# Between the two layers: more buffers for split weights, two weight splits inside the layer norm's chain, the keys' blocks split behind the queries', and the root's first guess in one operation

## The chip, the cores and the metric

The kernel runs on one core of one Trainium2 chip. The metric is the device time of one execution in microseconds (us). The kernel before takes 1261.22 us, the median of 3 runs (1261.05 to 1261.33). Its profile comes from one execution that took 1262.22 us itself.

## The reference

256 tokens of width 2048 pass through two layers in fp32. Layer 0 is a Mamba-2 SSD mixer, layer 1 a sparse-attention mixer with a lightning indexer. After each mixer comes a post-norm residual:

```
x = layer_norm(ALPHA * x + mixer(x), g, b)      # ALPHA = 4 ** 0.25
# layer 1 begins with
proj = x @ w_in                                  # 2048 -> 512 | 256 | 64 | 16 | 4096
c_q, c_kv, k_idx, w_idx, gate = split(proj)
c_q  = rms_norm(c_q, q_norm_g)                   # 512 columns, "queries"
c_kv = rms_norm(c_kv, kv_norm_g)                 # 256 columns, "keys"
```

Every product keeps fp32 precision: an operand is split into a rounded part `hi` and a remainder `lo`, and a product is made as hi·hi, hi·lo and lo·hi.

## The kernel before

**A stream of weight units.** `Stream` holds some 400 units of weights, each a tile of 128 x 1024 (128 x 672 for the keys), numbered in the order of use. `load` issues the DMA of unit i on SyncE's queue into one of 4 raw buffers. `convert` makes the two parts: ScalarE copies raw to `hi` with rounding (L98), VectorE subtracts to get `lo` (L99), and then the load of unit i + 4 is issued, into the raw buffer that the subtraction has just freed. `run` keeps the splits up to 4 units ahead of the matmuls; `limit` holds that back. The parts live in two pools of 4 buffers; a table `homes` sends single units to another pool, `wmore`, which in this kernel has 4 buffers of each part.

**The order is written out by hand.** Each engine executes its instructions in the order in which the program issues them, and waits on semaphores between engines. Nothing is scheduled by costs; what is issued first on an engine stands first in its queue, and a waiting instruction holds all behind it.

**Between the layers.** Units 160 to 223 are the output projection of layer 0 (`o1`), in four column blocks n of 512. Its last six units (218 to 223, `held`) are first multiplied for the token half 0 alone, so that the layer norm of half 0 can start on VectorE while TensorE does half 1 of those six. Units 224 to 231 (`wcq`) are the queries' projection, units 232 to 239 (`wkv`) the keys', and then come the gates' units (`wg`). The queries' units, too, are multiplied for half 0 first (`qp0`, six matmuls a unit) and, after all eight, for half 1 (`qp1`); the parts of all eight stay until then. `tail1` (L951) is issued with the last unit of `o1`, `early` (L973) after the matmuls of each queries' unit kb of half 0.

For one half the norm is this chain on VectorE: the residual of the last column block (L535), statistics (L538, L608, L609), the inverse root by an integer shift (L191), a guess (L193) and three steps of two operations each (L196, L198), and the normalization of four blocks of 512 columns in place (L927). Then TensorE transposes the half in four groups q of 512 columns (`turn`, tiles `x1t`), ScalarE applies gain and bias (`put`, L941, into tiles `x1f`), and each group is split into `x1T`: hi on ScalarE (L947) or VectorE (L945), lo on VectorE (L949). `x1T` is what the queries', keys' and gates' matmuls read. A name such as x1t10 means half 1, group 0; lo228 is the lo part of unit 228, the fifth queries' unit (kb 4).

After the queries comes `lat_norm` (copies of `qp`, statistics, its own root at L182), while TensorE multiplies the keys' units (tile `kvp`).

The kernel's end (`last`, L1039) is another layer norm of the same kind, whose root steps alternate with the operations that center the four blocks (L1056).

Of the kernel before, what the change touches and what calls it, by code (L numbers as in the profile page):

```python
# [53 lines left out]
LAST = 8  # L54
AHEAD = 2

# [8 lines left out]
class Stream:  # L65


    def __init__(self, nc, wraw, whi, wlo):
        self.nc, self.wraw, self.whi, self.wlo = nc, wraw, whi, wlo
        self.units, self.starts, self.active = [], {}, []  # L70
        self.raws, self.parts = {}, {}
        self.pos = self.ready = 0
        self.limit = 1 << 30
        self.homes = {}
# [14 lines left out]

    def convert(self, i, eng):  # L90

        if i < len(self.units):
            w = self.units[i].width
            r = self.raws.pop(i)
            ph, pl = (self.homes[i],) * 2 if i in self.homes else (self.whi, self.wlo)
            h = ph.tile([P, 1024], F32R, tag="hi", name=f"hi{i}")
            l = pl.tile([P, 1024], F32R, tag="lo", name=f"lo{i}")
            self.nc.scalar.activation(h[:, :w], r[:, :w], AF.Copy)  # L98
            eng.tensor_sub(l[:, :w], r[:, :w], h[:, :w].bitcast(F32))  # L99
            self.parts[i] = (h, l)  # L100
# [24 lines left out]
def trunk_kernel(ctx: ExitStack, tc: tile.TileContext, x, xt, w1, wdt, dtp, prm, wo1,  # L125
# [53 lines left out]
    def rsqrt(pool, dst, val, n, w, tag):  # L179

        t = pool.tile([n, w], F32, tag=tag, name=tag)
        v.tensor_scalar(t.bitcast(I32), val.bitcast(I32), 1, None, op0=ALU.logical_shift_right)  # L182
        v.tensor_scalar(dst.bitcast(I32), t.bitcast(I32), -1, MAGIC, op0=ALU.mult, op1=ALU.add)
        for k in range(3):
            v.tensor_mul(t, dst, dst)
            v.scalar_tensor_tensor(t, t, -0.5, val, op0=ALU.mult, op1=ALU.mult)
            v.scalar_tensor_tensor(dst, t, 1.5, dst, op0=ALU.add, op1=ALU.mult)

    def rsqrt1_steps(dst, val, t):

        v.tensor_scalar(t.bitcast(I32), val.bitcast(I32), 1, None, op0=ALU.logical_shift_right)  # L191
        yield
        v.tensor_scalar(dst.bitcast(I32), t.bitcast(I32), -1, MAGIC1, op0=ALU.mult, op1=ALU.add)  # L193
        for a in (A0, A1, A2):
# [419 lines left out]
    def stream_tok(kb, width, cell, name, held=None):  # L614
# [12 lines left out]
        def pe(h, l):  # L627
# [35 lines left out]
    def lat_norm(cell, width, g0, nt, name, dst):  # L663
# [4 lines left out]
        rs = d1.tile([P, 2], F32, tag=name + "r", name=name + "r")  # L668
        ps, tok, dst = cell["ps"], A[name], A[dst]
        for half in range(2):  # L670
# [12 lines left out]
        for q in range(nt // 2):  # L683
# [7 lines left out]
            for k in range(2):  # L691
                kt = 2 * q + k
                gs = par[:, g0 + kt:g0 + kt + 1]
                hi, lo = dst[:, kt, 0:T], dst[:, kt, T:2 * T]
                nc.scalar.activation(hi, pm[:, k * T:(k + 1) * T], AF.Copy, scale=gs)
# [221 lines left out]
    def normed(half, between=()):  # L917
# [18 lines left out]
    def put(half, q):  # L936
        t = d1.tile([P, 4, P], F32, tag="x1f", name=f"x1f{half}{q}", bufs=2)
        for j in range(4):
# [12 lines left out]
    def tail1(cell, held, mm):  # L951
# [41 lines left out]
    def area(*shape):  # L993
# [5 lines left out]
        elif len(shape) == 3:  # L999
# [4 lines left out]
             cb=area(384))  # L1004
    ckvT = d1.tile([P, 2, 2 * T], F32R, tag="ckvT", name="ckvT")
    cqT = d1.tile([P, 4, 2 * T], F32R, tag="cqT", name="cqT")
    A.update(ckvT=ckvT, cqT=cqT)
    mb = d1.tile([P, 384], F32, tag="mb", name="mb")
    nc.gpsimd.memset(A["cb"], 0.0)
# [177 lines left out]
```

## Time and profile before

| | |
|---|---|
| median of 3 runs | 1261.22 us |
| profiled execution | 1262.22 us |
| its span, first to last instruction | 1260.5 us |
| TensorE busy | 1235.4 us, 98% |
| VectorE busy | 909.4 us, 72% |
| ScalarE busy | 692.3 us, 55% |
| mean granted TensorE clock | 0.994 |
| stretch between the layers | about 670 to 732 us |

An idle time is printed in square brackets in front of the instruction that ended it, with what released it. Matmuls are pipelined, so that their durations overlap: how long one costs the engine is read from the distance between two starts. [...]

### The profile page before, as it was taken

How to read it: one execution, taken by the hardware profiler on the slowest of the kernel's cores; microseconds unless marked ns; L12 is line 12 of the kernel's file. 1: busy time of each engine (PE TensorE's matmuls, PEld its weight loads, DVE VectorE, ACT ScalarE, POOL GpSimd, SP SyncE). 2: the span in 40 equal slices, each digit the busy share in tenths (PEclk: the TensorE clock that was granted, in tenths of full speed). 3: DMA queues.
4: the chain of work that ended last, by engine and by line, in shares of the span. 5: the costliest groups of instructions: out<-in, count | busy, mean ns of one | idle time of the engine just before them, and what ended most of it. 6: DMA issues, size and time to landing. Idle time of an engine off the chain costs nothing.

```text
span 1260.5 us, 19096 instructions
## 1 busy us (share of the span) xinstructions
PE 1235.4 (98%) x7066; PEld 1072.6 (85%) x7066; DVE 909.4 (72%) x1685; ACT 692.3 (55%) x1186; POOL 68.6 (5%) x104
## 2 busy tenths in 40 slices
PE   8999999999999999999998999999999999999996
PEld 6888888888888888788887798999999999888885
DVE  6978788888889889757457568856666666567457
ACT  5566566666656666444435455566566666433340
POOL 1001001100110010110001000000000000000000
PEclk9999999999999999999999999999999999999998
DMA  7766657565656565676664464544444444965662
GB/s 273 207 189 184 205 177 216 156 214 178 215 167 208 184 203 171 193 255 192 202 198 159 157 225 149 185 152 149 160 159 145 154 149 151 352 204 185 200 197 86
DMA packets 65292, 236.51 MB, mean 188 GB/s; under 512 B 7912, under 2 KB 7920, under 8 KB 64816
## 3 DMA queue, kind: packets, MB, share of 16 engines
q1 hardware_dynamic: 60192, 215.12, 53.8%
q0 software_dynamic: 5008, 20.19, 5.0%
q8 instruction: 55, 0.90, 0.3%
q14 instruction: 37, 0.30, 0.1%
HBM read 231.00 MB, written 4.28 MB: 187 GB/s over the span
## 4 chain that ended last, share of the span: by engine, by line
PE 93%; DVE 4%; DMA 1%; issue 1%; ACT 0%; SPq 0%; DVEq 0%; ACTq 0%
PE acc L267 22%; PE acc L271 11%; PE g L267 9%; PE o L497 9%; PE o L499 9%; PE o L498 9%; PE g L271 5%; PE y L395 2%; DVE lo L99 1%; PE q L822 1%; PE q L823 1%; PE q L824 1%; PE lg L840 1%; PE o L871 1%; PE pt L864 1%; DMA scr<-in_xt_dram 1%
## 5 line engine op out<-in xcount | busy, mean ns | idle before, releaser
L99 DVE TENSOR_TENSOR lo<-raw,hi 128x1024 fp32r<-128x1024 f32 (+1 forms) x404 | 489.2, 1214 | 279.4 <-ACT hi L98 279.2
L98 ACT ACTIVATE hi<-raw 128x1024 fp32r<-128x1024 f32 (+1 forms) x404 | 421.2, 1049 | 219.6 <-PE o L499 163.0
L267 PE MATMUL acc<-xT,hi 128*128 128x512 f32 x1280 | 324.7, 395 | 0.0
L267 PEld LDWEIGHTS acc<-xT,hi 128*128 128x128 f32 x1280 | 230.3, 189 | 43.0 <-ACT E L350 0.9
L271 PEld LDWEIGHTS acc<-xT,lo 128*128 128x128 f32 x1280 | 174.5, 190 | 12.8
L271 PE MATMUL acc<-xT,lo 128*128 128x256 f32 x1280 | 178.3, 282 | 0.0
L267 PE MATMUL g<-x1T,hi 128*128 128x512 f32 x512 | 134.2, 404 | 0.0
L267 PEld LDWEIGHTS g<-x1T,hi 128*128 128x128 f32 x512 | 92.8, 188 | 17.9
L497 PE MATMUL o<-hi,yg 128*128 128x512 f32 x256 | 100.5, 393 | 0.8 <-DVE zs L278 0.8
L498 PE MATMUL o<-lo,yg 128*128 128x512 f32 x256 | 99.7, 389 | 0.0
L499 PE MATMUL o<-hi,yg 128*128 128x512 f32 x256 | 99.7, 389 | 0.0
L497 PE MATMUL o<-hi,og 128*128 128x512 f32 (+1 forms) x256 | 99.5, 389 | 0.0
L499 PE MATMUL o<-hi,og 128*128 128x512 f32 (+1 forms) x256 | 98.9, 386 | 0.0
L498 PE MATMUL o<-lo,og 128*128 128x512 f32 (+1 forms) x256 | 98.8, 386 | 0.0
L271 PEld LDWEIGHTS g<-x1T,lo 128*128 128x128 f32 x512 | 69.8, 190 | 5.1
L297 DVE SCALAR_TENSOR_TENSOR ca<-cr,convh,ca 128x255 f32<-128x255 f32 x144 | 69.3, 481 | 3.4
L271 PE MATMUL g<-x1T,lo 128*128 128x256 f32 x512 | 71.3, 282 | 0.0
L300 ACT ACTIVATE cr<-ca 128x256 f32<-128x256 f32 x48 | 20.1, 418 | 88.1 <-DVE ca L297 88.1
L497 PEld LDWEIGHTS o<-hi,yg 128*128 128x128 f32 x256 | 48.0, 188 | 11.2 <-ACT hi L98 1.3
L499 PEld LDWEIGHTS o<-hi,yg 128*128 128x128 f32 x256 | 48.1, 188 | 10.1
L498 PEld LDWEIGHTS o<-lo,yg 128*128 128x128 f32 x256 | 48.1, 188 | 9.9
L499 PEld LDWEIGHTS o<-hi,og 128*128 128x128 f32 x256 | 48.1, 188 | 9.9
(240 smaller groups left out, 1694.6 us busy)
## 6 DMA issues: line engine op xcount, KB each, us to landing
raw<-in_w_dram SPq DMA_DIRECT2D x160, 512.0 KB, 4.1
raw<-in_wo_dram SPq DMA_DIRECT2D x128, 512.0 KB, 4.3
raw<-in_wg_dram SPq DMA_DIRECT2D x64, 512.0 KB, 3.3
raw<-in_wab_dram SPq DMA_DIRECT2D x32, 512.0 KB, 3.3
abc<-acs_d POOLq DMA_DIRECT2D x32, 256.0 KB, 4.3
raw<-in_wcq_dram SPq DMA_DIRECT2D x8, 512.0 KB, 4.4
raw<-in_wkv_dram SPq DMA_DIRECT2D x8, 336.0 KB, 5.7
rx<-in_x_dram POOLq DMA_DIRECT2D x2, 1024.0 KB, 11.8
```

The costliest lines, as they stand in the source:

```text
L98: self.nc.scalar.activation(h[:, :w], r[:, :w], AF.Copy)
L99: eng.tensor_sub(l[:, :w], r[:, :w], h[:, :w].bitcast(F32))
L267: nc.tensor.matmul(ps, h[:, k * P:(k + 1) * P], xs[:, kt, :], start=(kt == 0), stop=False, skip_group_check=True)
L271: nc.tensor.matmul(ps[:, 0:T], l[:, k * P:(k + 1) * P], xs[:, kt, 0:T], start=False, stop=(kt == 15), skip_group_check=True)
L297: v.scalar_tensor_tensor(acc[:, d:], rw[:, :T - d], w(k), acc[:, d:], op0=ALU.mult, op1=ALU.add)
L300: nc.scalar.activation(rw, acc, AF.Tanh)
L395: nc.tensor.matmul(py[ks, c * T + s * P:(c + 1) * T], xsT[:, s, c, ks], ms[c][k][:, ws], start=(c == 0 and s == 0), stop=(s == 1), skip_gr ...
L497: nc.tensor.matmul(ps, ah, hs, start=(kk == 2 * first), stop=False)
L498: nc.tensor.matmul(ps, ah, ls, start=False, stop=False)
L499: nc.tensor.matmul(ps, al, hs, start=False, stop=(kk == 31))
L822: nc.tensor.matmul(ps, h[:, o:o + P], cqT[:, kt, 0:T], start=(kt == 0), stop=False)
L823: nc.tensor.matmul(ps, h[:, o:o + P], cqT[:, kt, T:2 * T], start=False, stop=False)
```

## The change

It consists of six edits.

1. `wmore` gets 6 buffers of each part in place of 4, and holds units 222 to 227, then 232 and 233; `AHEAD` grows from 2 to 4, so that units 226 and 227 may be split before and at the head of `tail1`. The space for it comes from the `x1f` tiles, which now lie in the dead part of the residual's input, and from `ckvT`, `cqT` and `mb`, which are made later, in a pool `lat` opened once `wmore` is closed.
2. In `tail1` units 228 and 229 are split on either side of the residual of half 1, and 230 and 231 inside the norm of half 1: `start` issues the ScalarE part, `finish` the VectorE part and the load. `convert` is cut in two for that.
3. The normalization of half 1 is shared: blocks 0 and 2 on VectorE, 1 and 3 on ScalarE, with a new one-column operation for the bias (`nm`).
4. The hi parts of the transposed groups 0 and 1 are made on VectorE, of 2 and 3 on ScalarE (before: 1 and 3, 0 and 2).
5. The transposes of half 1 stand behind the seventh and eighth queries' unit (kb 6 and 7) in place of the sixth and seventh; the first two keys' units are split ahead of that half's groups, and two more right behind the queries, ahead of `lat_norm`.
6. The root's shift and guess become one operation (val x -0.5 + constant on the integer view), in both root functions, so also at the kernel's end.

```diff
-AHEAD = 2
+AHEAD = 4
...
-    def convert(self, i, eng):
+    def convert(self, i, eng, later=False):
...
             self.nc.scalar.activation(h[:, :w], r[:, :w], AF.Copy)
-            eng.tensor_sub(l[:, :w], r[:, :w], h[:, :w].bitcast(F32))
             self.parts[i] = (h, l)
+            self.halfway[i] = (l[:, :w], r[:, :w], h[:, :w].bitcast(F32))
+        if not later:
+            self.finish(i, eng)
+
+    def finish(self, i, eng):
+        if i in self.halfway:
+            eng.tensor_sub(*self.halfway.pop(i))
         self.load(i + RAW)
...
-        v.tensor_scalar(t.bitcast(I32), val.bitcast(I32), 1, None, op0=ALU.logical_shift_right)
-        yield
-        v.tensor_scalar(dst.bitcast(I32), t.bitcast(I32), -1, MAGIC1, op0=ALU.mult, op1=ALU.add)
+        v.tensor_scalar(dst.bitcast(I32), val.bitcast(I32), -0.5, MAGIC1, op0=ALU.mult,
+                        op1=ALU.add)
...
-    wmore = between.enter_context(tc.tile_pool(name="wmore", bufs=4))
-    for i in (n_o1 - 2, n_o1 - 1, n_o1, n_o1 + 1, n_o1 + 6, n_o1 + 7):
-        st.homes[i] = wmore
+    wmore = between.enter_context(tc.tile_pool(name="wmore", bufs=6))
+    for i in (-2, -1, 0, 1, 2, 3, 8, 9):
+        st.homes[n_o1 + i] = wmore
...
                 for a in held:
                     mm(*a, 1)
+                st.limit = 1 << 30
+                st.convert_to(n_o1 + EARLY + 4)
...
+        nm = d1.tile([P, 1], F32, tag="nm", name="nm")
+        v.scalar_tensor_tensor(nm, mv[:, 0:1], -1.0, rs, op0=ALU.mult, op1=ALU.mult)
         for n in range(4):
             s = L["r"][:, half, n * 512:(n + 1) * 512]
-            v.tensor_scalar(s, s, mv[:, 0:1], rs, op0=ALU.subtract, op1=ALU.mult)
+            if n % 2:
+                nc.scalar.activation(s, s, AF.Identity, scale=rs, bias=nm)
+            else:
+                v.tensor_scalar(s, s, mv[:, 0:1], rs, op0=ALU.subtract, op1=ALU.mult)
...
-        if q % 2:
+        if q < 2:
             v.tensor_copy(hi, t)
...
-        st.limit = n_o1 + EARLY
-        st.convert_to(n_o1 + 3)
+        st.limit = n_o1 + EARLY + 2
+        st.convert_to(n_o1 + AHEAD)
         now(put(0, 0))
         now(put(0, 1))
-        st.convert_to(n_o1 + 4)
+        st.convert_to(n_o1 + AHEAD + 1)
         now(residual(3, 1, cell))
+        st.convert_to(n_o1 + 6)
         p2, p3 = put(0, 2), put(0, 3)
-        normed(1, (p2, p2, p3, p3))
+
+        def split():
+            st.start(n_o1 + 6)
+            st.start(n_o1 + 7)
+            yield
+            st.finish(n_o1 + 6, v)
+        normed(1, (p2, p2, p3, p3, split()))
+        st.finish(n_o1 + 7, v)
```

VectorE's queue, from the end of half 1's root on, before; `rx` holds the residual stream, `mv1` and `rs1` mean and inverse root of half 1:

```order
L196 TENSOR_SCALAR t1_6920<-rs1_6918,ve1_6919 128x1
L198 SCALAR_TENSOR_TENSOR rs1_6918<-t1_6920,rs1_6918 128x1
L927 TENSOR_SCALAR rx_6159<-rx_6159,mv1_6917,rs1_6918 128x512 x4
L99 TENSOR_TENSOR lo228_6970<-raw228_6784,hi228_6969 128x1024
L99 TENSOR_TENSOR lo229_6982<-raw229_6796,hi229_6981 128x1024
L99 TENSOR_TENSOR lo230_6994<-raw230_6892,hi230_6993 128x1024
L99 TENSOR_TENSOR lo231_7006<-raw231_6912,hi231_7005 128x1024
L949 TENSOR_TENSOR x1T_6831<-x1f10_7033,x1T_6831 128x4x128
```

Lo228 to lo231 stand behind the whole norm of half 1. The same place now, the end of half 1's root on VectorE:

```order
L207 TENSOR_SCALAR t1_6925<-rs1_6923,ve1_6924 128x1
L209 SCALAR_TENSOR_TENSOR rs1_6923<-t1_6925,rs1_6923 128x1
L106 TENSOR_TENSOR lo230_6945<-raw230_6804,hi230_6944 128x1024
L946 SCALAR_TENSOR_TENSOR nm_6956<-mv1_6922,rs1_6923 128x1
L952 TENSOR_SCALAR rx_6155<-rx_6155,mv1_6922,rs1_6923 128x512 x2
L106 TENSOR_TENSOR lo231_6948<-raw231_6893,hi231_6947 128x1024
L106 TENSOR_TENSOR lo232_7007<-raw232_6911,hi232_7006 128x672
L106 TENSOR_TENSOR lo233_7019<-raw233_6920,hi233_7018 128x672
L970 CAST x1T_6832<-rx_6155 128x4x128
L974 TENSOR_TENSOR x1T_6832<-rx_6155,x1T_6832 128x4x128
```

Lo228 and lo229 have moved ahead of the root, lo230 stands between root and normalization, and the first two keys' units stand ahead of the first group of half 1. VectorE at the residual of half 0, before; `o1_3_0` is the last column block's sum for half 0:

```order
L99 TENSOR_TENSOR lo225_6793<-raw225_6748,hi225_6792 128x1024
L535 SCALAR_TENSOR_TENSOR rx_6159<-rx_6159,o1_3_0_6568 128x512
L538 BN_STATS st1_6160<-rx_6159 128x6 x2
L608 BN_AGGR mv0_6813<-st1_6160 128x2
L609 TENSOR_SCALAR ve0_6815<-mv0_6813 128x1
L191 TENSOR_SCALAR t0_6816<-ve0_6815 128x1
L193 TENSOR_SCALAR rs0_6814<-t0_6816 128x1
```

and now:

```order
L106 TENSOR_TENSOR lo225_6789<-raw225_6744,hi225_6788 128x1024
L106 TENSOR_TENSOR lo226_6801<-raw226_6756,hi226_6800 128x1024
L546 SCALAR_TENSOR_TENSOR rx_6155<-rx_6155,o1_3_0_6564 128x512
L549 BN_STATS st1_6156<-rx_6155 128x6 x2
L621 BN_AGGR mv0_6815<-st1_6156 128x2
L622 TENSOR_SCALAR ve0_6817<-mv0_6815 128x1
L203 TENSOR_SCALAR rs0_6816<-ve0_6817 128x1
```

Lo226 has moved ahead of the residual, from behind the normalization of half 0, and the root begins with one operation. Further on, between that normalization and the residual of half 1, VectorE now has lo227, two casts, two subtractions and lo228, where it had lo226, lo227, one cast and two subtractions; lo229 stands right behind the residual's statistics. ScalarE around half 1's groups, before (`x1t10` is the transposed group 0 of half 1):

```order
L98 ACTIVATE hi228_6969<-raw228_6784 128x1024
L98 ACTIVATE hi229_6981<-raw229_6796 128x1024
L98 ACTIVATE hi230_6993<-raw230_6892 128x1024
L98 ACTIVATE hi231_7005<-raw231_6912 128x1024
L941 ACTIVATE x1f10_7033<-x1t10_7023,par_88 128x128 x4
L947 ACTIVATE x1T_6831<-x1f10_7033 128x4x128
```

and now (the target `rx` of L966 is the `x1f` of before):

```order
L98 ACTIVATE hi230_6944<-raw230_6804 128x1024
L98 ACTIVATE hi231_6947<-raw231_6893 128x1024
L950 ACTIVATE rx_6155<-rx_6155,nm_6956,rs1_6923 128x512 x2
L98 ACTIVATE hi232_7006<-raw232_6911 128x672
L98 ACTIVATE hi233_7018<-raw233_6920 128x672
L966 ACTIVATE rx_6155<-x1t10_7030,par_88 128x128 x4
```

The two operations of the normalization and the keys' two splits now stand between hi231 and the first group. On TensorE the only difference is that x1t10 and x1t11 stand behind unit 230 and x1t12 and x1t13 behind unit 231, right ahead of `qp1`.

## Rows read from the trace of the kernel before

**Rows 1.** The page, part 1: busy time of each engine, share, instructions.
```profile
PE 1235.4 (98%) x7066; PEld 1072.6 (85%) x7066; DVE 909.4 (72%) x1685; ACT 692.3 (55%) x1186; POOL 68.6 (5%) x104
```

**Rows 2.** Who TensorE waited for, 500 to 800 us: total us, times, longest.
```profile
PE qp L624 <- DVE lo L99: 4.2, 1, 4.2
PE kvp L623 <- ACT hi L98: 1.3, 1, 1.3
```

**Rows 3.** Windows: length, each engine's busy us (instructions), granted clock, DMA share, GB/s.
```profile
688.50:692.75 4.25, 0.00 (x2) 0.00 (x1) 4.07 (x12) 1.95 (x3) 0.57 (x1) 0.85 0.00 0
692.75:697.60 4.85, 4.85 (x11) 3.68 (x12) 3.35 (x3) 0.00 (x0) 0.00 (x0) 0.50 0.99 382
713.50:716.20 2.70, 0.89 (x3) 0.44 (x3) 1.82 (x3) 2.45 (x4) 0.00 (x0) 1.00 0.00 0
```

**Rows 4.** Timeline of TensorE: start, us, operation, count, idle before and releaser.
```profile
678.06 1.03 PE L933 MATMUL x1t<-ident,rx 128*128 128x128 f32 x8
678.85 0.48 PE L497 MATMUL o<-hi,yg 128*128 128x512 f32 x1
...
682.59 0.40 PE L623 MATMUL qp<-hi,x1T 128*128 128x512 f32 x1
...
688.11 0.39 PE L623 MATMUL qp<-hi,x1T 128*128 128x512 f32 x1
692.75 0.79 PE L624 MATMUL qp<-lo,x1T 128*128 128x512 f32 x1 [4.25 <-DVE lo L99]
...
697.61 1.37 PE L933 MATMUL x1t<-ident,rx 128*128 128x128 f32 x8
698.73 0.48 PE L623 MATMUL qp<-hi,x1T 128*128 128x512 f32 x1
```

**Rows 5.** Timeline of TensorE from the last queries' matmul to the keys' first.
```profile
713.32 0.40 PE L625 MATMUL qp<-hi,x1T 128*128 128x512 f32 x1
715.05 0.42 PE L623 MATMUL kvp<-hi,x1T 128*128 128x336 f32 x1 [1.34 <-ACT hi L98]
715.95 0.42 PE L624 MATMUL kvp<-lo,x1T 128*128 128x336 f32 x1 [0.47 <-DVE lo L99]
```

**Rows 6.** Timeline of VectorE between the layers.
```profile
672.79 0.69 DVE L535 SCALAR_TENSOR_TENSOR rx<-rx,o 128x512 f32<-128x512 f32 x1 [0.27 <-PE o L499]
...
676.79 1.92 DVE L927 TENSOR_SCALAR rx<-rx,mv,rs 128x512 f32<-128x512 f32 x4
...
684.50 0.68 DVE L535 SCALAR_TENSOR_TENSOR rx<-rx,o 128x512 f32<-128x512 f32 x1
...
687.33 0.42 DVE L945 CAST x1T<-x1f 128x512 fp32r<-128x512 f32 x1
...
689.64 1.92 DVE L927 TENSOR_SCALAR rx<-rx,mv,rs 128x512 f32<-128x512 f32 x4
691.48 4.62 DVE L99 TENSOR_TENSOR lo<-raw,hi 128x1024 fp32r<-128x1024 f32 x4
700.78 0.69 DVE L949 TENSOR_TENSOR x1T<-x1f,x1T 128x512 fp32r<-128x512 f32 x1 [4.68 <-ACT x1T L947]
```

**Rows 7.** Timeline of ScalarE between the layers.
```profile
670.20 1.06 ACT L98 ACTIVATE hi<-raw 128x1024 fp32r<-128x1024 f32 x1 [1.58 <-DMA raw<-in_wcq_dram]
674.17 1.06 ACT L98 ACTIVATE hi<-raw 128x1024 fp32r<-128x1024 f32 x1 [2.91 <-PE o L499]
678.69 1.51 ACT L941 ACTIVATE x1f<-x1t,par 128x128 f32<-128x128 f32 x4 [3.46 <-PE x1t L933]
...
700.12 0.63 ACT L947 ACTIVATE x1T<-x1f 128x512 fp32r<-128x512 f32 x1
...
714.25 2.71 ACT L98 ACTIVATE hi<-raw 128x672 fp32r<-128x672 f32 x4
```

**Rows 8.** The chain that ended last, at the kernel's end: start, us, operation.
```profile
1250.34 0.17 DVE t L191
1250.53 0.15 DVE rs L193
```

More of the change, by code (lines that the diff above doesn't have):

```diff
@@ L70, in __init__ @@
         self.units, self.starts, self.active = [], {}, []
-        self.raws, self.parts = {}, {}
+        self.raws, self.parts, self.halfway = {}, {}, {}
         self.pos = self.ready = 0
@@ L98, in convert, with start @@
             self.nc.scalar.activation(h[:, :w], r[:, :w], AF.Copy)
-            eng.tensor_sub(l[:, :w], r[:, :w], h[:, :w].bitcast(F32))
             self.parts[i] = (h, l)
+            self.halfway[i] = (l[:, :w], r[:, :w], h[:, :w].bitcast(F32))
[4 more added lines that the diff above has]
+            eng.tensor_sub(*self.halfway.pop(i))
         self.load(i + RAW)
+    def start(self, i):
+        assert i == self.ready
+        self.convert(i, None, later=True)
+        self.ready += 1
     def convert_to(self, end, eng=None):
@@ L181, in rsqrt @@
         t = pool.tile([n, w], F32, tag=tag, name=tag)
-        v.tensor_scalar(t.bitcast(I32), val.bitcast(I32), 1, None, op0=ALU.logical_shift_right)
-        v.tensor_scalar(dst.bitcast(I32), t.bitcast(I32), -1, MAGIC, op0=ALU.mult, op1=ALU.add)
+        v.tensor_scalar(dst.bitcast(I32), val.bitcast(I32), -0.5, MAGIC, op0=ALU.mult,
+                        op1=ALU.add)
         for k in range(3):
@@ L189, in rsqrt1_steps @@
     def rsqrt1_steps(dst, val, t):
-        v.tensor_scalar(t.bitcast(I32), val.bitcast(I32), 1, None, op0=ALU.logical_shift_right)
-        yield
-        v.tensor_scalar(dst.bitcast(I32), t.bitcast(I32), -1, MAGIC1, op0=ALU.mult, op1=ALU.add)
+        v.tensor_scalar(dst.bitcast(I32), val.bitcast(I32), -0.5, MAGIC1, op0=ALU.mult,
+                        op1=ALU.add)
         for a in (A0, A1, A2):
@@ L592, in trunk_kernel @@
     between = ExitStack()
-    wmore = between.enter_context(tc.tile_pool(name="wmore", bufs=4))
-    for i in (n_o1 - 2, n_o1 - 1, n_o1, n_o1 + 1, n_o1 + 6, n_o1 + 7):
-        st.homes[i] = wmore
+    wmore = between.enter_context(tc.tile_pool(name="wmore", bufs=6))
+    for i in (-2, -1, 0, 1, 2, 3, 8, 9):
+        st.homes[n_o1 + i] = wmore
     rx = big.tile([P, 4, D], F32, tag="A", name="rx")
     L["r"], L["x"] = rx[:, 0:2, :], rx[:, 2:4, :]
+    x1f = [rx[:, 2 + k, 0:512].rearrange("p (j t) -> p j t", j=4) for k in range(2)]
     L["st"] = d1.tile([P, 2, 8, 6], F32, tag="st", name="st1")
@@ L668, in lat_norm @@
         rs = d1.tile([P, 2], F32, tag=name + "r", name=name + "r")
-        ps, tok, dst = cell["ps"], A[name], A[dst]
+        ps, tok = cell["ps"], A[name]
         for half in range(2):
@@ L693, in lat_norm @@
                 gs = par[:, g0 + kt:g0 + kt + 1]
-                hi, lo = dst[:, kt, 0:T], dst[:, kt, T:2 * T]
+                hi, lo = A[dst][:, kt, 0:T], A[dst][:, kt, T:2 * T]
                 nc.scalar.activation(hi, pm[:, k * T:(k + 1) * T], AF.Copy, scale=gs)
@@ L924, in normed @@
             now(step)
+        if half == 0:
+            for n in range(4):
+                s = L["r"][:, half, n * 512:(n + 1) * 512]
+                v.tensor_scalar(s, s, mv[:, 0:1], rs, op0=ALU.subtract, op1=ALU.mult)
+            return
+        nm = d1.tile([P, 1], F32, tag="nm", name="nm")
+        v.scalar_tensor_tensor(nm, mv[:, 0:1], -1.0, rs, op0=ALU.mult, op1=ALU.mult)
         for n in range(4):
             s = L["r"][:, half, n * 512:(n + 1) * 512]
-            v.tensor_scalar(s, s, mv[:, 0:1], rs, op0=ALU.subtract, op1=ALU.mult)
+            if n % 2:
+                nc.scalar.activation(s, s, AF.Identity, scale=rs, bias=nm)
+            else:
+                v.tensor_scalar(s, s, mv[:, 0:1], rs, op0=ALU.subtract, op1=ALU.mult)
     def turn(half, q):
@@ L936, in put @@
     def put(half, q):
-        t = d1.tile([P, 4, P], F32, tag="x1f", name=f"x1f{half}{q}", bufs=2)
+        t = x1f[q % 2]
         for j in range(4):
@@ L963, in tail1 @@
         mm(*held[5], 1)
-        st.limit = n_o1 + EARLY
-        st.convert_to(n_o1 + 3)
+        st.limit = n_o1 + EARLY + 2
+        st.convert_to(n_o1 + AHEAD)
         now(put(0, 0))
         now(put(0, 1))
-        st.convert_to(n_o1 + 4)
+        st.convert_to(n_o1 + AHEAD + 1)
         now(residual(3, 1, cell))
+        st.convert_to(n_o1 + 6)
         p2, p3 = put(0, 2), put(0, 3)
-        normed(1, (p2, p2, p3, p3))
+        def split():
[5 more added lines that the diff above has]
+        st.finish(n_o1 + 7, v)
     def early(kb):
-        if kb == 5:
+        if kb == 6:
             turn(1, 0)
@@ L977, in early @@
             now(put(1, 0))
-        elif kb == 6:
+            now(put(1, 1))
+        elif kb == 7:
             turn(1, 2)
             turn(1, 3)
-            now(put(1, 1))
-        elif kb == 7:
             now(put(1, 2))
             now(put(1, 3))
-            st.limit = 1 << 30
+            st.convert_to(n_o1 + EARLY + 2)
     L.update(tail1=tail1, early=early)
@@ L1004, in trunk_kernel @@
              cb=area(384))
[L1005 to L1008, printed above, removed]
     nc.gpsimd.memset(A["cb"], 0.0)
@@ L1019, in trunk_kernel @@
     nc.gpsimd.dma_start(x1_d, L["r"])
+    st.run(n_o1 + EARLY + 2)
     between.close()
+    lat = ctx.enter_context(tc.tile_pool(name="lat", bufs=1))
+    ckvT = lat.tile([P, 2, 2 * T], F32R, tag="ckvT", name="ckvT")
+    cqT = lat.tile([P, 4, 2 * T], F32R, tag="cqT", name="cqT")
+    A.update(ckvT=ckvT, cqT=cqT)
+    mb = lat.tile([P, 384], F32, tag="mb", name="mb")
     heads = ExitStack()
```

## The prediction

> **What bounds the kernel now.** I read the page's first part, then TensorE's waits, then the granted clock in windows around them, then the three engines' timelines between the layers. TensorE is busy for 1235.4 us, 98% of the span [rows 1], so a gain has to be TensorE time that is lost. Between the layers its waits are one of 4.2 us for a lo part (unit 228, the fifth queries' block) and a short pair at the first keys' block [rows 2]. [...]
>
> The price of both in starts: at full rate a queries' matmul takes 0.23 (24 of them, four blocks, from 682.59 to 688.11, so 1.38 a block) and eight transposes 0.79 (678.06 to 678.85) [rows 4].
> - The stop: 688.11 to 692.75 is 4.64 for one matmul, 4.41 lost.
> - The low clock: 692.75 to 697.61 holds 11 matmuls, 4.86 in place of 2.53, so 2.33 lost; eight transposes take 1.12 (697.61 to 698.73), 0.33 lost. Together 2.66.
> - The keys' start: 713.32 to 715.05 is 1.73 for one matmul (1.50 lost), 715.05 to 715.95 is 0.90, where by the idle time printed 0.47 was waiting; with the slower first matmul I count 0.85 [rows 5].
>
> In all 4.41 + 2.66 + 2.35 = 9.42 us lost.
>
> The cause of the first stands on VectorE: lo228 starts at 691.48, behind the whole norm of half 1, whose residual starts at 684.50 and whose normalization begins at 689.64 [rows 6]. TensorE wanted lo228 at 688.3. The second comes from ScalarE, which makes the keys' first four hi parts from 714.25 on, after the queries [rows 7].
>
> **The change part by part.** *Lo226 ahead of half 0's residual.* This adds a wait to VectorE's queue, and behind it stands the norm that TensorE's first transposes need. Hi226 can start when hi225 is done, 670.20 + 1.06 = 671.3, if raw226 has landed; before, ScalarE already waited for raw225's DMA there, and hi226 only started at 674.17 because its buffer was held [rows 7]. No row shows raw226's landing. Its load is issued one split (1.15, from 4.62 for four [rows 6]) behind raw225's, so I take a start of 671.9; the bounds are 671.3 and 673. Then 1.06 for hi, 1.23 for lo, and the residual starts at 674.2 where it started at 672.79: 1.4 later (0.8 to 2.5). One root operation less gives 0.19 back (below). The normalization then starts at 676.79 - 0.19 + 1.4 = 678.0, and its first block is done 0.54 later, at 678.5. TensorE gets there at 678.06. **Added: 0.5** (0 to 1.6). TensorE's queries start at 683.1 in place of 682.59.
>
> *The way to half 1's residual.* VectorE: three more blocks at 0.46, then lo227 to 681.0. ScalarE starts the first group's x1f 0.63 behind its transposes, as at 678.69 against 678.06: 679.2, and two groups of 1.5 end at 682.2. VectorE's cast and subtraction of group 1 end their slots at 683.3, lo228 follows (hi228 is done at about 683.25), and the residual starts at 684.45. That is where it started before; lo228 is now ahead of it, ready at 684.5, and TensorE wants it at 683.1 + 4 x 1.38 + 0.23 = 688.85. **The stop of 4.41 and its low clock go**, if nothing else is late.
>
> *What is late next on VectorE.* From the residual to the end of the root it was 689.64 - 684.50 = 5.14. One root operation goes (0.19), one cast goes to ScalarE (a slot of 0.33), lo229 enters (1.15): 5.77. Lo230 starts at 690.2 and is done at 691.45; TensorE wants it at 683.1 + 6 x 1.38 + 0.23 = 691.6. No wait, by 0.15. Then the new one-column operation and two blocks; lo231 is done at about 693.5 and wanted at 683.1 + 7 x 1.38 + 0.79 + 0.23 = 693.8. No wait, by 0.3. These two have no slack: each microsecond by which VectorE is later becomes one of TensorE. I allow 0 to 1.
>
> *Half 1's groups.* The normalization on ScalarE is not in the trace. The nearest rows are a copy of 512 columns (0.63) and four operations with scale and bias on 128 each (1.51) [rows 7]; I take 0.63, since it is one instruction over SBUF, and keep 1.5 as the other end. From 691.55 two end at 692.8. The keys' two hi parts follow at 0.68 each (2.71 for four), to 694.2. Only then comes x1t10's group, 1.51 to 695.7, the cast on VectorE 0.42, to 696.2, and the subtraction 0.69, to 696.9. TensorE has done eight blocks and sixteen transposes at 683.1 + 8 x 1.38 + 2 x 0.79 = 695.7, and its next matmul needs that hi, its third that lo. **Added: 0.5 + 0.2 = 0.7** (0.2 to 2.4, where the upper end has ScalarE's two operations at 1.5). The old place of x1t10 had a block and a half of cover; now there is one.
>
> *The keys.* Their first two units are split by 695.3 and wanted at about 707.6, so **1.50 + 0.85 go**. The next two wait for the buffers of units 228 and 229, free when the fifth and sixth blocks of half 1 are multiplied, some 4 us ahead of the keys' start, and are wanted 3.7 us behind it. The loads of raw230 to raw235 stand on SyncE's queue behind lo226 to lo231, all of which come earlier, so the transfers that fill the 692.75 window (0.99 of the DMA engines [rows 3]) spread out. The statistics of the queries lose the four splits that stood inside them. I price nothing here; the cover is the keys' 15 us of matmuls.
>
> *The root in one operation.* In the chain at the end the shift starts at 1250.34 and the guess at 1250.53 [rows 8]: 0.19 goes. The new operation is of the guess's kind; its duration could be that of any small one, 0.15 to 0.27. The four roots of layer 0 and the two of the latents lie under matmuls and count as nothing.
>
> **The sum.** 9.42 + 0.19 - 0.5 - 0.7 = 8.4 us. The profiled execution took 1262.22 (span 1260.5 and 1.7 around it), so it would take 1253.8. That execution is 1.0 above the median of 1261.22; I forecast **1252.8** for the median.
>
> **The rivals.** *A, the clock falls again.* Two new stops of 0.5 and 0.7 stand 17 us apart. If one takes the clock to 0.50, it costs what it cost before, 2.66: 1255.5. Against it: the pair of 1.34 and 0.47 left the clock at 1.00 [rows 3]. [...]
>
> *B, the stop moves to lo230 or to x1t10.* VectorE's queue has no gap from 679 to 694 in my working, and ScalarE's hardly one. If half 0's residual is at its late end and the new ScalarE operations at theirs, the added waits are 1.6, 1.0 and 2.4, less the 1.2 already counted: 3.8 more, 1256.6. For it: margins of 0.15 and 0.3. Half of that is likelier, about 1254.7.
>
> *C, slower.* The clock falls at the wait ahead of half 1's matmuls and stays down for that whole pass: 48 matmuls at 0.20 extra (0.43 in place of 0.23) are 9.6, so the gain of 8.4 turns into a loss of 1.2: 1262.4 as a median. It decides from about 42 slow matmuls on. Against it: after a stop of 4.25, far longer, the clock was back after 4.85 us.
>
> *D, the change doesn't do what it says.* If raw228 or its buffer came late, lo228 would still be late, but its load follows lo224, which is done ahead of the residual at 672.79 [rows 6], and its buffer is free ahead of the transposes at 678.06 [rows 4], so that would take 4 us of delay. Then only the keys' 2.35 remain, less 1.2: about 1260.
>
> **How the numbers follow.** My forecast with its own range of 1251.6 (nothing added) to 1254.2 has 0.68; A 0.10, B 0.14, D 0.03, C 0.05. The range of 1251.6 to 1256.2 takes in the bounds, A and most of B. A measurement of this kernel tells 0.2%, 2.5 us, from no change. Forecast, A and B are all faster by more than that, and half of D: 0.93; same 0.02; slower 0.05.
>
> **What would show it.** Right: no wait of TensorE for lo228; granted clock 1.00 from 688 to 698; the first keys' matmul within 0.3 of the last queries' one; half 0's residual on VectorE 1 to 2 us later; a short wait at the first transposes and one ahead of the first matmul of half 1; the first keys' matmul about 24.4 us behind the first queries' one, where it was 715.05 - 682.59 = 32.5. Wrong: a wait above 1 us for lo230, lo231 or x1T, or a clock of 0.50 anywhere between the layers.

## The result and the profile after

The changed kernel takes 1254.14 us (median of 6 runs, 1253.45 to 1255.36) where the kernel before, beside it, takes 1261.36: a ratio of 0.994 (95% interval 0.9929 to 0.9951), 7.2 us faster. A second comparison, in the experiments, gave 1253.32 against 1260.89, a ratio of 0.9939 (0.9927 to 0.9952). The forecast was 1252.8 in a range of 1251.6 to 1256.2. The profiled execution took 1254.12 us over a span of 1252.4, 8.1 less of each than before.

Page, part 1, answering to [rows 1]; then who TensorE waited for between the layers, answering to [rows 2].

```profile
PE 1232.8 (98%) x7066; PEld 1072.0 (86%) x7066; DVE 906.6 (72%) x1674; ACT 693.3 (55%) x1188; POOL 67.9 (5%) x104
```

```profile
PE x1t L958 <- DVE rx L943: 1.2, 1, 1.2
PE o L508 <- DVE zs L289: 0.8, 1, 0.8
```

Both old waits, for lo228 and at the keys, are gone. The first row is new: the first transposes (`x1t`) wait for half 0's norm. The second lies ahead of this stretch and is no part of the change. The windows answer to [rows 3]: the first two cover the old stop and the old low clock, the third the keys' start at its new place.

```profile
688.50:692.75 4.25, 4.25 (x20) 3.52 (x19) 4.11 (x12) 2.96 (x4) 0.00 (x0) 1.00 0.28 81
692.75:697.60 4.85, 4.74 (x29) 3.59 (x27) 4.13 (x6) 4.85 (x12) 0.57 (x1) 1.00 0.74 214
707.50:709.50 2.00, 2.00 (x13) 1.88 (x12) 0.92 (x2) 1.16 (x3) 0.00 (x0) 1.00 0.78 241
```

Granted clock 1.00 in all three. TensorE is busy for 4.25 of 4.25 us where it stood still before, and the second window holds 29 instructions where 11 ran before. TensorE's timeline, answering to [rows 4, 5]:

```profile
677.74 0.39 PE L510 MATMUL o<-hi,yg 128*128 128x512 f32 x1
679.30 1.11 PE L958 MATMUL x1t<-ident,rx 128*128 128x128 f32 x8 [1.17 <-DVE rx L943]
...
683.90 0.40 PE L636 MATMUL qp<-hi,x1T 128*128 128x512 f32 x1
...
695.71 1.04 PE L958 MATMUL x1t<-ident,rx 128*128 128x128 f32 x8
696.85 0.50 PE L636 MATMUL qp<-hi,x1T 128*128 128x512 f32 x1
697.18 0.40 PE L637 MATMUL qp<-lo,x1T 128*128 128x512 f32 x1
697.57 0.50 PE L638 MATMUL qp<-hi,x1T 128*128 128x512 f32 x1
...
707.91 0.39 PE L638 MATMUL qp<-hi,x1T 128*128 128x512 f32 x1
708.14 0.31 PE L636 MATMUL kvp<-hi,x1T 128*128 128x336 f32 x1
...
723.75 2.00 PE L278 MATMUL g<-x1T,hi 128*128 128x512 f32 x8
```

The last matmul ahead of the transposes starts at 677.74, so they could have started at 677.97 and start 1.33 late. Eight transposes take 0.79, but half 1's first matmul comes 1.14 behind the last eight; it and its next three starts lose 0.72 together. The keys start 0.23 behind the last queries' matmul, with no loss.

VectorE and ScalarE, answering to [rows 6, 7]: VectorE to the first normalization, then half 1's; below it ScalarE.

```profile
673.76 1.23 DVE L106 TENSOR_TENSOR lo<-raw,hi 128x1024 fp32r<-128x1024 f32 x1 [1.24 <-ACT hi L98]
674.90 0.68 DVE L546 SCALAR_TENSOR_TENSOR rx<-rx,o 128x512 f32<-128x512 f32 x1
...
678.70 1.92 DVE L943 TENSOR_SCALAR rx<-rx,mv,rs 128x512 f32<-128x512 f32 x4
...
684.01 1.22 DVE L106 TENSOR_TENSOR lo<-raw,hi 128x1024 fp32r<-128x1024 f32 x1
685.14 0.68 DVE L546 SCALAR_TENSOR_TENSOR rx<-rx,o 128x512 f32<-128x512 f32 x1
...
690.78 1.23 DVE L106 TENSOR_TENSOR lo<-raw,hi 128x1024 fp32r<-128x1024 f32 x1
```

```profile
672.66 1.06 ACT L98 ACTIVATE hi<-raw 128x1024 fp32r<-128x1024 f32 x1 [1.40 <-DMA raw<-in_wcq_dram]
...
692.12 1.52 ACT L950 ACTIVATE rx<-rx,nm,rs 128x512 f32<-128x512 f32 x2 [1.29 <-DVE nm L946]
693.55 1.40 ACT L98 ACTIVATE hi<-raw 128x672 fp32r<-128x672 f32 x2
```

Lo226 (the first row) waits for hi226, which waits for raw226's DMA until 672.66; the residual behind it starts 2.1 later than in [rows 6]. The first transposes start 6.64 behind hi226 (672.66 to 679.30). Lo228 starts at 684.01, where it started at 691.48.

Where the time went, in starts lost against an even pace (0.2275 a queries' matmul, 0.155 a keys', 0.79 eight transposes; "clock" terms of the queries at 0.23, as in the prediction), each worked out from the TensorE timeline of one execution. The matmul behind every eight transposes loses 0.09 in every kernel, which is left out where nothing else is lost there. "Stretch" is from the moment TensorE reaches the first transposes to the first gates' matmul. The numbers in brackets are those of the experiments below:

| kernel | first transposes | queries, half 0's and lo parts | half 1's first | keys' start | stretch |
|---|---|---|---|---|---|
| before | 0 | 4.41 + 2.66 clock | 0 | 2.35 | 53.87 |
| before, second profile | 0 | 4.40 + 1.69 clock | 0 | 2.33 | 52.87 |
| changed | 1.33 | 0 | 0.72 | 0 | 45.78 |
| changed, second profile | 1.33 | 0 | 0.72 | 0 | 45.76 |
| one split ahead, in before (1) | 0.25 | 4.1 + 3.1 clock | 0 | 2.35 + 1.5 clock | 55.29 |
| lo parts behind the norm (2) | 1.58 | 3.2 + 1.6 clock | 3.7 + 1.6 clock | 0 | 55.51 |
| keys' splits behind the queries (3) | 1.33 | 0 | 0 | 2.33 + 1.46 clock | 49.06 |
| lo226 behind the norm (5) | 0.06 | 0.83 | 0.85 | 0 | 45.51 |
| keys behind the groups (6) | 1.72 | 0 | 0 | 0 | 45.49 |
| both (7) | 0 | 0 | 0 | 0 | 43.75 |
| norm on VectorE (8) | 1.49 | 0.50 | 0.10 | 0 | 46.11 |
| root in two operations (9) | 1.41 | 0 | 0.83 | 0 | 46.00 |

### The profile page after: what moved, and what is told of

The parts are those of the page before. It is cut to its first block, busy times and chain, and to the rows that moved or that the text cites. A ratio compares the mean times of both kernels' runs of the same rounds, so it can differ in the third digit from the quotient of the medians.

```text
span 1252.4 us, 19083 instructions
## 1 busy us (share of the span) xinstructions
PE 1232.8 (98%) x7066; PEld 1072.0 (86%) x7066; DVE 906.6 (72%) x1674; ACT 693.3 (55%) x1188; POOL 67.9 (5%) x104
## 4 chain that ended last, share of the span: by engine, by line
PE 93%; DVE 4%; issue 1%; ACT 1%; DMA 1%; DVEq 0%; SPq 0%; ACTq 0%
PE acc L278 22%; PE acc L282 11%; PE g L278 9%; PE o L508 9%; PE o L509 9%; PE o L510 9%; PE g L282 5%; PE y L406 2%; DVE lo L106 1%; PE q L837 1%; PE q L839 1%; PE q L838 1%; PE lg L855 1%; PE o L886 1%; PE pt L879 1%
```

## The experiments

Diffs are against the changed kernel, except where said.

**1. One more split ahead of half 1's norm, in the kernel before** (diff against that). Is it the order on VectorE that makes the stop?

```diff
-        st.convert_to(n_o1 + 4)
+        st.convert_to(n_o1 + 5)
         now(residual(3, 1, cell))
```

> The kernel before, but unit 228 is split ahead of the residual of half 1 (one number changed). Theory (a split moved ahead of the norm moves the stop by one block; all four have to go between the chain's steps): no wait for lo228, half 1's residual 1.15 us later, lo229 ready at 693.8 where it is wanted at 689.7: a stop of 4 us, clock 0.50 behind it, time within 0.5 us of the kernel before. Rival (the stop was lo228's place alone): 5 us or more below the kernel before.

1262.56 us, ratio to before 1.0009 (0.9999 to 1.0018). TensorE around the stop:

```profile
689.66 0.40 PE L623 MATMUL qp<-hi,x1T 128*128 128x512 f32 x1
693.97 0.80 PE L624 MATMUL qp<-lo,x1T 128*128 128x512 f32 x1 [3.91 <-DVE lo L99]
```

One split ahead only moves the stop one block on (688.11 to 689.66 for the last matmul ahead of it), at nearly the old length. The median lies 1.5 above the 1261.07 of the kernel before beside it, where 0.5 was expected: in the profile the clock stayed at 0.50 up to 699.8, and stood at 0.50 again from 717 to 720, behind the keys' pair. So the stop is the whole norm standing ahead of a queue of lo parts, and moving one of them isn't enough. Whether two or three would do was not tried.

**2. All four lo parts behind the norm again, in the changed kernel.** Everything else stays.

```diff
-        st.convert_to(n_o1 + AHEAD + 1)
+        st.start(n_o1 + 4)
         now(residual(3, 1, cell))
-        st.convert_to(n_o1 + 6)
+        st.start(n_o1 + 5)
...
-            st.finish(n_o1 + 6, v)
         normed(1, (p2, p2, p3, p3, split()))
-        st.finish(n_o1 + 7, v)
+        for i in range(4, 8):
+            st.finish(n_o1 + i, v)
```

> The changed kernel, but VectorE's halves of the splits of units 228 to 231 (and the loads behind them) stand behind the normalization of half 1 again, ScalarE's halves where the change put them. Theory (the old stop was the place of lo228 behind the norm): TensorE waits for lo228 again; on VectorE the norm is done at about 691.5, since its second subtraction waits for ScalarE's last copy at 688.9, lo228 at 692.7, wanted at 689.6: a stop of 3.0 us, less the 0.5 us saved at half 1's first matmuls, so 2.5 us more than the changed kernel, and 5.2 us if the clock falls in it. Rival (half the normalization on ScalarE, the shorter root and the cast given to ScalarE have removed the stop by themselves): no wait above 1 us for lo228, time as the changed kernel's.

1262.71 us, ratio 1.0011 (1.0001 to 1.002): the whole gain is gone, and more than was expected. TensorE's two stops; below, ScalarE:

```profile
691.90 0.80 PE L637 MATMUL qp<-lo,x1T 128*128 128x512 f32 x1 [3.06 <-DVE lo L106]
...
703.80 0.50 PE L636 MATMUL qp<-hi,x1T 128*128 128x512 f32 x1 [3.12 <-DVE x1T L970]
```

```profile
700.38 1.51 ACT L98 ACTIVATE hi<-raw 128x672 fp32r<-128x672 f32 x2 [9.03 <-DMA raw<-in_wkv_dram]
701.80 2.54 ACT L966 ACTIVATE rx<-x1t,par 128x128 f32<-128x128 f32 x7
```

The first stop is the one of before, shorter by 1.2. The second I had not counted: `finish` also issues the load of the unit four further on. The four keys' loads leave SyncE from 691.91 on, right behind the 2 MB write of the residual (GpSimd, 691.65), and take 7.9 us at the median from issue to landing, where the same four of the changed kernel take 3.1. ScalarE waits for the first in front of half 1's group, and TensorE for the group. Both stops are followed by a clock of 0.50 (692 to 694, and 706 to 708). So moving the lo parts is what brings the gain: the stretch is 9.7 longer here than in the changed kernel, and about half of that stands at the second stop. That half needs edit 5 as well. In the kernel before, the same four loads are about as late (issued from 692.72 on, 7.3 us at the median) and cost nothing, because there the keys' splits stand behind the queries; with the splits ahead of half 1's groups, late loads become a stop. The loads were not moved apart from the lo parts.

**3. The keys' splits behind the queries again.**

```diff
                 st.limit = 1 << 30
-                st.convert_to(n_o1 + EARLY + 4)
...
-        st.limit = n_o1 + EARLY + 2
+        st.limit = n_o1 + EARLY
```

> The changed kernel, but the keys' units are split behind the queries' matmuls and the copies of their sums, as before the change. Theory: the keys' start costs 1.50 + 0.85 us again (waits of 1.3 for hi and 0.5 for lo), half 1's first group is 0.5 us earlier: 1.8 us more than the changed kernel. Rival (with the loads earlier ScalarE makes the first keys' part in the gap anyway): less than 0.8 us more.

1257.4 us, ratio 0.9967 (0.9954 to 0.998). The waits are those of [rows 5] to the hundredth, but the clock isn't. TensorE, then windows from 709 on:

```profile
708.97 0.42 PE L636 MATMUL kvp<-hi,x1T 128*128 128x336 f32 x1 [1.34 <-ACT hi L98]
709.86 0.42 PE L637 MATMUL kvp<-lo,x1T 128*128 128x336 f32 x1 [0.47 <-DVE lo L106]
```

```profile
710.00:711.00 1.00, 1.00 (x6) 1.00 (x7) 1.00 (x2) 0.87 (x2) 0.00 (x0) 0.77 0.32 48
711.00:712.00 1.00, 1.00 (x5) 1.00 (x4) 1.00 (x2) 0.00 (x0) 0.00 (x0) 0.50 0.78 280
713.00:716.00 3.00, 3.00 (x19) 3.00 (x18) 2.69 (x12) 1.20 (x2) 0.00 (x0) 0.84 0.78 256
```

The pair loses 2.33 in starts and the low clock behind it 1.46 more. Half 1's 0.72 goes at the same time, so the stretch is 3.28 longer than in the changed kernel (49.06), 3.07 of it by these three, not 1.8. Taken out of the changed kernel, the keys' edit is worth more than the 2.35 - 0.7 that I had given it, by the low clock; in the kernel before, whose clock stayed at 1.00 behind the pair, its worth stays at that.

**4. The same two kernels again, for the clock.** In experiment 1, too, the same pair (1.34, 0.47) was followed by a clock of 0.50 (717 to 720), where before it had stayed at 1.00.

> The kernel before again, for its granted clock alone. Its first keys' matmuls waited 1.34 and 0.47 us and the clock stayed at 1.00 behind them; in two experiments with the same pair at the same place of the program (1.34 and 0.47) the clock fell to 0.50 some 0.9 us behind it. Theory 1, it differs from execution to execution of one kernel: here the clock may be at 0.50 somewhere in the 6 us behind the pair, and then the keys' matmuls there cost about 1 to 1.5 us more. Theory 2, it is fixed by what the kernel does around the pair: 1.00 again, as in the first profile.

> The changed kernel with the keys' first units split behind the queries, again. In its first profile the clock stood at 1.00 until 710, 0.50 from 711 to 713 and 1.00 again from 716, behind waits of 1.34 and 0.47. Theory 1 (from execution to execution): the clock may stay at 1.00 here. Theory 2 (fixed by the kernel): 0.50 for 3 to 4 us again, beginning some 0.9 us behind the pair.

One execution each: 1260.67 us (the kernel before) and 1256.47 us (experiment 3). Windows of the kernel before, then of experiment 3, from 0.9 and from 0.1 us behind the pair's second matmul on:

```profile
715.00:716.00 1.00, 1.00 (x8) 1.00 (x8) 1.00 (x2) 0.11 (x1) 0.00 (x0) 1.00 0.89 226
716.00:717.00 1.00, 1.00 (x9) 1.00 (x8) 0.90 (x6) 0.01 (x1) 0.00 (x0) 1.00 1.00 374
```

```profile
709.00:710.00 1.00, 1.00 (x4) 1.00 (x5) 1.00 (x2) 0.94 (x2) 0.00 (x0) 0.56 0.20 30
710.00:711.00 1.00, 1.00 (x5) 1.00 (x5) 1.00 (x2) 0.00 (x0) 0.00 (x0) 0.50 0.87 282
```

Before stayed at 1.00 twice, experiment 3 fell twice (0.7 us behind the pair's second matmul, and 0.2 us behind it, by the mean clock of the windows in which it fell), experiment 1 fell. By these five profiles it goes with the kernel more than with the execution; what sets it was not shown, and I leave it open. This second profile of before also gave what the forecast lacked: how much the low clock behind the same stop varies. Below, the window in which the clock comes back, in the first profile, then in the second:

```profile
698.00:699.00 1.00, 1.00 (x9) 1.00 (x8) 0.00 (x0) 0.42 (x2) 0.00 (x0) 0.86 0.52 122
```

```profile
695.00:696.00 1.00, 1.00 (x4) 0.76 (x4) 0.26 (x1) 0.00 (x0) 0.00 (x0) 0.66 0.83 295
```

The first was at 0.50 from inside the stop of 4.25 until 698.3, 5.5 behind its end. The second, behind a stop of 4.24, was at 0.50 from 692.3 to 695.7 only, until 3.8 behind the stop's end. Its span is 1258.7 against 1260.5.

**5. Lo226 behind half 0's norm again; 6. the keys' first splits behind half 1's groups; 7. both.** Do the two new waits come from where I put them?

```diff
-    st.limit = n_o1 + AHEAD
+    st.limit = n_o1 + 2
```

```diff
-        st.limit = n_o1 + EARLY + 2
+        st.limit = n_o1 + EARLY
...
             now(put(1, 1))
+            st.limit = n_o1 + EARLY + 2
+            st.convert_to(n_o1 + EARLY + 2)
```

> The changed kernel, but lo226 stands behind the normalization of half 0 again. Theory (half 0's residual is late because lo226 waits there for hi226, whose raw block lands at 672.7): the residual starts at 672.8 in place of 674.9, TensorE's wait of 1.2 us at the first transposes is gone, the queries start at 682.6 in place of 683.9, and no other wait of TensorE passes 1 us; about 0.2 us is given back ahead of half 1's matmuls, so 1.0 to 1.2 us less than the changed kernel. Rival (VectorE's queue is full, so what is moved behind the norm comes back as a wait for lo230 or lo231): a wait of 1 us or more at units 230 or 231, time as the changed kernel's.

> The changed kernel, but the first two keys' units are split behind groups 0 and 1 of half 1, not ahead of them. Theory (the keys' two hi parts on ScalarE hold up the first group): ScalarE starts the first group about 0.8 us earlier against its transposes, the 0.5 us that TensorE loses at the first matmuls of half 1 (0.35 + 0.16 in starts) goes, the keys still start without a wait: 0.5 us less than the changed kernel. Rival (the first group itself, x1f, cast and subtraction, is what TensorE waits for): the 0.5 us stay, time unchanged; second rival: groups 2 and 3 are now late, a wait in the middle of half 1's pass.

> Both edits at once. Theory: the two waits are separate and both go, TensorE runs from 655 to 724 without a wait above 0.3 us: 1.6 to 1.8 us less than the changed kernel, about 1252.4 where that takes 1254.1. Rival: with the queries starting 1.3 us earlier VectorE and ScalarE are late somewhere else, and less than 1.2 us is won.

> The changed kernel unaltered, beside its variants on the same chip. Both theories: 0.994 of the kernel before, some 7 to 8 us less.

| kernel | us (lowest to highest) | ratio to before (interval) |
|---|---|---|
| 5, lo226 behind the norm | 1252.79 (1251.9 to 1253.82) | 0.9935 (0.9922 to 0.9947) |
| 6, keys behind the groups | 1253.37 (1252.22 to 1254.06) | 0.9937 (0.9923 to 0.995) |
| 7, both | 1252.2 (1251.69 to 1253.13) | 0.9932 (0.9919 to 0.9944) |
| changed kernel beside them | 1253.32 (1252.7 to 1253.93) | 0.9939 (0.9927 to 0.9952) |

5 takes the first wait away, and most of it comes back as small losses from the fifth block on, as its rival had it, though in waits below 0.5. Its TensorE, with the place where lo230 is now late:

```profile
677.28 1.11 PE L958 MATMUL x1t<-ident,rx 128*128 128x128 f32 x8
...
691.05 0.50 PE L637 MATMUL qp<-lo,x1T 128*128 128x512 f32 x1 [0.17 <-DVE lo L106]
...
695.84 0.50 PE L636 MATMUL qp<-hi,x1T 128*128 128x512 f32 x1 [0.23 <-DVE x1T L970]
```

6 takes the 0.72 at half 1 away, and in its profile the first transposes cost 0.39 more. Its ScalarE shows why: hi225 and hi226 both stand for their DMA, hi226 0.6 later than in the changed kernel.

```profile
671.97 1.06 ACT L98 ACTIVATE hi<-raw 128x1024 fp32r<-128x1024 f32 x1 [2.21 <-DMA raw<-in_wcq_dram]
673.26 1.06 ACT L98 ACTIVATE hi<-raw 128x1024 fp32r<-128x1024 f32 x1 [0.23 <-DMA raw<-in_wcq_dram]
```

With both, TensorE loses nothing between the layers, and the stretch is 2.03 shorter, the whole 1.33 + 0.72 and just above the expectation. The two alone bring 0.27 and 0.29. They are not simply additive. The traces suggest two reasons, which no run isolates. In 5, lo225 starts at 671.74 (in 7 at 671.26), behind a raw225 that landed later, while TensorE reached the transposes earlier (677.22 against 678.03): VectorE's normalization leads TensorE's arrival by 0.54 in place of 1.43, and the 0.9 less of lead seems to come back as waits. And the late lo231 and keys' splits that remain in 5 stand ahead of half 1's groups on both engines. 7 is the fastest kernel tried. By medians it is 1.1 us ahead of the changed one; their intervals overlap, so by time alone the step is likely and not certain, and the trace is what shows it. The medians of 5 (0.5 below the changed kernel) and of 6 (level with it) set neither apart from it.

**8. The whole normalization on VectorE.**

```diff
-            if n % 2:
-                nc.scalar.activation(s, s, AF.Identity, scale=rs, bias=nm)
-            else:
-                v.tensor_scalar(s, s, mv[:, 0:1], rs, op0=ALU.subtract, op1=ALU.mult)
+            v.tensor_scalar(s, s, mv[:, 0:1], rs, op0=ALU.subtract, op1=ALU.mult)
```

(`nm` goes too.)

> The changed kernel, but VectorE normalizes all four blocks of half 1, and the one-column operation for the bias is gone. Theory (the two engines' queues trade the same wait): VectorE is 0.8 us later for lo231, a wait of about 0.4 us at unit 231, ScalarE makes the keys' parts during the norm and the 0.5 us at half 1's first matmuls shrink to 0.2: within 0.3 us of the changed kernel. Rival (sharing the normalization carries a part of the gain): 0.8 us or more above it.

1253.28 us, ratio 0.9935 (0.9919 to 0.9952): as the changed kernel. Half 1's first matmuls lose 0.10 in place of 0.72, but 0.50 comes back one block earlier, where lo231 is late:

```profile
694.50 0.48 PE L636 MATMUL qp<-hi,x1T 128*128 128x512 f32 x1
695.12 0.50 PE L637 MATMUL qp<-lo,x1T 128*128 128x512 f32 x1
```

This sharing of the norm brings nothing here.

**9. The root in two operations again.**

```diff
-        v.tensor_scalar(dst.bitcast(I32), val.bitcast(I32), -0.5, MAGIC1, op0=ALU.mult,
-                        op1=ALU.add)
+        v.tensor_scalar(t.bitcast(I32), val.bitcast(I32), 1, None, op0=ALU.logical_shift_right)
+        yield
+        v.tensor_scalar(dst.bitcast(I32), t.bitcast(I32), -1, MAGIC1, op0=ALU.mult, op1=ALU.add)
```

> The changed kernel with the root's shift and guess as two operations again. Theory: 0.19 to 0.21 more in the chain at the kernel's end, where 4.32 before and 4.11 in the changed kernel stood between the root's first operation and the copy that ends the chain: 4.3 here. Between the layers the two roots lie ahead of the normalizations that end TensorE's waits: about 0.2 more at the first transposes (1.17 there in the changed kernel), and 0 to 0.2 at half 1's. In all 0.2 to 0.6. Rival: the new operation is no shorter than the two together, since the second started in the shadow of the first; then the end chain is 4.1 again.

One execution, 1254.22 us. VectorE's end chain in the changed kernel, then here (last column's variance, then the root):

```profile
1242.24 0.15 DVE L1081 TENSOR_SCALAR ve<-mv 128x1 f32<-128x1 f32 x1
1242.43 0.15 DVE L203 TENSOR_SCALAR rs<-ve 128x1 int32<-128x1 int32 x1
1242.62 0.27 DVE L207 TENSOR_SCALAR t<-rs,ve 128x1 f32<-128x1 f32 x1
```

```profile
1242.15 0.15 DVE L1082 TENSOR_SCALAR ve<-mv 128x1 f32<-128x1 f32 x1
1242.33 0.15 DVE L203 TENSOR_SCALAR t<-ve 128x1 int32<-128x1 int32 x1
1242.52 0.15 DVE L205 TENSOR_SCALAR rs<-t 128x1 int32<-128x1 int32 x1
1242.59 0.74 DVE L1091 SCALAR_TENSOR_TENSOR fin<-fin,mv 128x512 f32<-128x512 f32 x1
```

The new operation is of 0.15 and follows at the same 0.19. From `ve` to the last scaling it is 4.03 in the changed kernel (1246.27) and 4.22 here (1246.37): 0.19. Between the layers the stretch is 0.22 longer here, and the first transposes start 6.83 behind hi226 in place of 6.64: 0.19 again. By this one profile the edit is worth about 0.4, half of it at the end.

Edit 4 and the later place of half 1's transposes (in edit 5) were not undone by themselves, so what they bring is open.

## Why the prediction was right, and where its sizes were off

**The stop and its low clock.** Right: no wait for lo228, clock 1.00 throughout. Experiments 1 and 2 show that the order of the four lo parts makes the stop; and experiment 2 that the loads tied to them count as well once the keys' splits stand ahead of half 1's groups. The prediction named these loads and took them for nothing ("I price nothing here"); in the changed kernel, where they are early, that holds.

**The size of the low clock, and the median.** The term was 2.66 from one execution (clock 0.50 in the second window of [rows 3]). The second profile of before gave 1.69 after the same stop. I took the 1.0 by which the profiled execution lay above the median off the forecast too (1253.8 to 1252.8), as if it stood outside what the change removes. By the second profile that excess is of the size of the longer low clock, which the change removes with the rest. The times on record agree: of 20 executions of the kernel before, run beside experiments 1, 2, 3 and 8, the twelve with a mean granted clock of 0.996 have a median span of 1259.05, the four with 0.994, which is the clock of the first profile (span 1260.5), one of 1260.45. Left at 1253.8, the forecast would have been 0.3 from the 1254.14 measured. This is the step that was mis-sized most, along with the next. Rival C's argument that the clock was back after 4.85 us rests on the same single profile: there it was back 5.5 behind the stop's end, in the second 3.8.

**The first transposes.** The wait was forecast at 0.5 from hi226 at 671.9; hi226 started at 672.66, and 1.33 was lost (bounds 0 to 1.6). The load of raw226 was indeed issued 1.14 behind that of raw225, but it landed 2.46 behind it (672.64 against 670.18), since it took 4.6 us and the other 3.3. The trace of before had this already: raw226 is issued there at 668.03 and landed at 672.52. In the second profile hi226 started at 672.26, TensorE was 0.40 earlier too, and the loss was again 1.33. The cause is right by experiments 5 and 7: without lo226 there, the loss is 0.06 or 0. It is right in its sizes, too: in all seven profiles with lo226 in this place and the new root the first transposes start 6.63 to 6.65 behind hi226, so that the loss (1.19 to 1.72) is set by when raw226 lands, against TensorE's own arrival.

**Half 1's first matmul.** 0.7 forecast, 0.72 lost; experiments 6 and 7 take it away by moving the keys' splits. That the sizes meet is in part luck. The ScalarE normalization is 0.76 an operation, not 0.63, but TensorE came 0.8 later than forecast (696.50 in place of 695.7), the group on ScalarE 0.7; the wait for hi was 0.35 in place of 0.5, and the next three starts lost 0.37 in place of 0.2.

**Margins at lo230 and lo231.** No loss in the changed kernel. That they have little slack was right: experiments 5 and 8 lose about 0.5 there.

**Keys and root.** The first keys' matmul stands 24.24 behind the first queries' one (24.4 forecast), and 0.23 behind the last. The root gave 0.20 in the chain at the end (4.23 before, 4.03 now, from the variance to the last scaling).

**The sum** in the profiled pair: 9.42 - 1.33 - 0.72 + 0.20 = 7.57 by named losses; the spans differ by 8.1. Another 0.7 lies within the stretch. 0.43 of it is at the first four of the eight transposes of the queries' latents (`qt`), which stand among the keys' matmuls; first before, then in the changed kernel:

```profile
721.49 0.95 PE L689 MATMUL qt<-ident,sC 128*128 128x128 f32 x4
```

```profile
713.64 0.60 PE L704 MATMUL qt<-ident,sC 128*128 128x128 f32 x4
```

From the keys' matmul ahead of these four to the one behind them it is 0.94 before and 0.51 in the changed kernel. Before, their weight loads wait twice, 0.5 in all, for the latents that VectorE normalizes (`sC`); in the changed kernel they don't. The prediction had seen that the queries' statistics lose the four splits that stood inside them, and had priced nothing. The keys' matmuls themselves, but for the pair, take the same in both (14.43 and 14.44). The rest, about 0.3, is spread over the queries' matmuls. No run isolates either. And 0.25 goes the other way behind the stretch: from the first gates' matmul to the last column's variance it is 518.49 in the changed kernel and 518.22 before (518.49 and 518.24 in the second profiles), which uses up what the root gives at the end; its cause is open. So the gain of the profiled pair, 8.1 for 8.4, is near by luck in part: 0.8 more was lost at the first transposes, and about as much came from terms that had no price.

**The rivals.** A did not come, but its counter-argument was weaker than its 0.10 made it: the pair of 1.34 and 0.47 left the clock at 1.00 in both profiles of before and was followed by 0.50 in experiments 1 and 3 and in the second profile of 3. The changed kernel's two losses of 1.33 and 0.72 left it at 1.00 in both its profiles, as did those of experiments 6, 8 and 9 (1.72; 1.49 and 0.50; 1.41 and 0.83). B, C and D did not come; in experiment 2, whose stops of 3.06 and 3.12 lie at lo228 and x1t10, a clock of 0.50 followed each of them, which B had left out: 9.7 in the stretch.

## What to carry to other kernels

Before you move an operation, list what is issued with it: put back behind the norm, the lo parts held up the loads as well, and with the keys' splits in their new place these cost about as much as the lo parts. Before you take a landing from the distance of two issues, read it from the trace: the load behind another one landed later than that (2.46 for 1.14). When you take one wait away, look at the next consumer in the queue: experiment 5 took 1.27 off the first transposes and lost 0.83 and 0.13 more behind them. Look for the set of edits that leaves the queue a lead (here two that bring 0.3 each alone and 2.0 together in the traces, 0.5, nothing and 1.1 by the medians). If the profiled execution lies above the median, ask whether the excess is part of what the change removes before you take it off the forecast.

## What the runs showed of the hardware

At a granted clock of 1.00 the queries' matmuls started 0.227 us apart (changed kernel, 684.83 to 693.21), at 0.50 0.428 (kernel before, 693.76 to 697.18). The same pair of waits (1.34 and 0.47) left the granted clock at 1.00 in two profiles of one kernel (before) and was followed by 0.50 in three of two others (experiment 1, and experiment 3 twice). After stops of 4.25 and 4.24 in the same kernel (before) the clock came back 5.5 and 3.8 us behind the stop's end. In four profiles in which lo226 stands ahead of the residual (the changed kernel twice, experiments 6 and 9) the load that hi226 waits for (512 KB) took 4.48 to 4.98 us from issue to landing. The same four 336 KB loads took 3.1 us at the median in the changed kernel, and 7.9 in experiment 2, where all four were issued right behind a 2 MB write.
